# Low parts of the attention's weights: from a subtraction on VectorE to an adding transfer, with a lead of two slots

## The chip, the cores and the metric

The kernel runs on one core of a Trainium2 chip. The metric is the device time of one execution in microseconds; of several executions the median is taken. Each profile is one execution taken by the hardware profiler.

## The reference

Two decoder layers work on one sequence of 512 tokens with 1024 features, all in float32. Each layer has four residual updates in this order; the mixers share one input projection.

```
x = x + 0.5 * swiglu(rms_norm(x, norm_ffn1[l]), ...)
h = rms_norm(x, norm_mix[l])
proj = h @ w_in[l]                      # columns: RWKV-7 | attention | convolution
y_rwkv = rwkv7_mixer(token_shift(proj[..., :1280], shift_mu[l]), ...)
y_attn = attention_mixer(proj[..., 1280:2432], q_norm, k_norm)
y_conv = conv_mixer(proj[..., 2432:], ...)
x = x + concat(y_rwkv, y_attn, y_conv) @ w_out[l]
x = x + 0.5 * swiglu(rms_norm(x, norm_ffn2[l]), ...)
```

The attention has six heads of 64 features and three dilated windows; q and k are normalised per head before the scores. The change concerns the 1152 columns of `w_in` that give the attention's v, k and q.

## The kernel before, in words

**Products in three passes.** The dense products run on TensorE (PE) in float32r. So that little accuracy is lost, each weight tile and each activation is split into a high part, which is the value rounded to float32r, and a low part, which is the value minus its high part. A product is then three matmuls added up in one PSUM bank: high by high, high by low, low by high (`mm3`, lines 124 to 126; for the attention's columns lines 874 to 876, where the low weight stands in line 875 and is the second of the three).

**A slot.** Weights come in slots of up to 128 x 1024 float32, made by `slot` (lines 105 to 119). A slot has three tiles, `raw`, `hi` and `lo`, each out of a ring of three buffers. SyncE (SP) loads `raw` from HBM (L112), ScalarE (ACT) casts it into `hi` (L113). The low part is made in one of two ways. In the plain way VectorE (DVE) subtracts `hi` from `raw` (L118). In the adding way ACT writes the negated high part into `lo` (L115), and a transfer that GpSimd (POOL) issues adds `raw` to it (L116).

```
if add:
    nc.scalar.activation(lo[:, :cols], hi[:, :cols].bitcast(F32), AF.Copy, scale=-1.0)
    nc.gpsimd.dma_start(out=lo[:, :cols], in_=raw[:, :cols], accum_op=ALU.add)
else:
    nc.vector.tensor_tensor(lo[:, :cols], raw[:, :cols], hi[:, :cols].bitcast(F32), op=ALU.subtract)
```

**The feed of the mixer.** The two feed-forward parts of a layer make their slots where they use them, the plain way. The mixer in between takes its slots from the generator `feed`, which knows the whole list in advance: 14 slots of 1024 columns for the RWKV and convolution projections (numbers 0 to 13), 12 slots of 768 columns for the attention (numbers 14 to 25; four each for v, k and q in the order of the list w = 1, 0, 2), and then the slots of the output projection. `WADD` says which numbers are made in the adding way, and up to where the feed stays two slots ahead of the consumer; behind that it stays one ahead:

```
for i, a in enumerate(srcs):
    got.append(self.slot(*a, WADD[0] <= i < WADD[1]))
    if len(got) > (2 if i < WADD[1] else 1):
        yield got.pop(0)
        if len(got) > 1 and i >= WADD[1]:
            yield got.pop(0)
```

**The mixer's order.** Each layer's mixer first runs the columns of slots 0 to 13, and between them the preparation of the RWKV recurrence on DVE, ACT and POOL. Then DVE inverts small triangular blocks in a chain of 60 dependent steps (`inverses`, L585 and L591), ends it with a copy (L594), and SP writes the result to HBM and loads it back rearranged into the tiles `EB` (L564). The recurrence itself goes over eight chunks (`p3`, `p4`, `s1` to `s4`, lines 642 to 706), each a chain of small matmuls with short DVE and ACT steps in between. To keep PE busy between these, dense work is mixed in by `step`: first the attention's columns (`att_cols`), later the attention itself (`att_core`), the convolution's end and the output projection.

`att_cols` goes through three groups of four slots. Each group fills four PSUM banks; for the first two groups ACT then reads each bank twice, a square into one scratch tile (L898) and a scaled copy `nat` (L899), DVE reduces the square (L900, L901), and POOL raises to a power (L902) and multiplies (L904). The next group needs the banks that ACT has read. PE transposes the normalised tiles in `turn` (L854), while the slots after it run. At the lowest priority DVE runs the 30 taps of the convolution (L1008).

**What sets the order.** The program is a list of instructions with priorities in program order; before the run a scheduler orders each engine's queue once, by priority and by when it expects each instruction to be ready. On the chip each queue is worked off in that order.

Of the kernel before, what the change touches and what calls it, by code (L numbers as in the profile page):

```python
# [25 lines left out]
XPAD = 56  # L26
SCRATCH = 2048
CPOS = 4
WADD = (3, 14)
CO = (1, 1)  # L30
TURN = 2
PRE = 8
# [50 lines left out]
class Kern:  # L83
# [202 lines left out]
    def feed(self, srcs):  # L286

        got = []
# [6 lines that stand above are left out]
# [844 lines left out]
```

## Time and profile before

| what | value |
|---|---|
| median of 3 runs | 2071.73 us (2071.52 to 2076.33) |
| the profiled execution | 2076.13 us |
| its span, first to last instruction | 2074.4 us |
| mean granted TensorE clock | 0.989 |
| subtractions on DVE (L118) | 346, 470.6 us |
| negations on ACT (L115) and adding transfers on POOL (L116) | 22 each |

An instruction's time is in us from the start of the span. A line of a timeline has the start, the duration, the engine, the line of the kernel and the tiles written and read; the number in brackets is the idle time of the engine before it and what ended that. PE's matmuls overlap, so their start-to-start distance, not their duration, is what they cost. The first layer's mixer lies at about 340 to 710 us, the second's at about 1370 to 1730.

### The profile page before, as it was taken

How to read it: one execution, taken by the hardware profiler on the slowest of the kernel's cores; microseconds unless marked ns; L12 is line 12 of the kernel's file. 1: busy time of each engine (PE TensorE's matmuls, PEld its weight loads, DVE VectorE, ACT ScalarE, POOL GpSimd, SP SyncE). 2: the span in 40 equal slices, each digit the busy share in tenths (PEclk: the TensorE clock that was granted, in tenths of full speed). 3: DMA queues.
4: the chain of work that ended last, by engine and by line, in shares of the span. 5: the costliest groups of instructions: out<-in, count | busy, mean ns of one | idle time of the engine just before them, and what ended most of it. 6: DMA issues, size and time to landing. Idle time of an engine off the chain costs nothing. (4 is left out here: it accounts for less than half of the span.)

```text
span 2074.4 us, 26095 instructions
## 1 busy us (share of the span) xinstructions
PE 2033.6 (98%) x10406; PEld 1652.5 (80%) x10406; DVE 1095.8 (53%) x1543; ACT 766.4 (37%) x1158; POOL 345.3 (17%) x320
## 2 busy tenths in 40 slices
PE   8999999989999999999999999999999999999999
PEld 6888888767867788888888888887688678888887
DVE  5545433597866545543345454336887664554422
ACT  4323322564365323323233232226634553233221
POOL 3101101232411201110011011002424111110100
PEclk9999999999999999999999999999999899999999
DMA  4232333534312333323323323335333132323332
GB/s 169 92 102 92 97 109 124 131 92 112 85 44 92 103 102 92 100 89 101 97 92 101 102 92 97 112 120 132 95 102 91 34 105 92 100 94 102 99 109 66
DMA packets 85033, 205.34 MB, mean 99 GB/s; under 512 B 26992, under 2 KB 32624, under 8 KB 84912
## 3 DMA queue, kind: packets, MB, share of 16 engines
q1 hardware_dynamic: 81312, 191.79, 29.8%
q0 software_dynamic: 3168, 11.54, 2.8%
q8 instruction: 81, 1.33, 0.3%
q10 hardware_dynamic: 432, 0.36, 0.1%
q14 instruction: 40, 0.33, 0.1%
HBM read 183.47 MB, written 8.65 MB: 93 GB/s over the span
## 5 line engine op out<-in xcount | busy, mean ns | idle before, releaser
L113 ACT CAST hi<-raw 128x1024 fp32r<-128x1024 f32 (+3 forms) x368 | 350.8, 954 | 981.4 <-PE psg L125 854.1
L124 PE MATMUL psg<-xh,hi 128*128 128x512 f32 x1632 | 644.1, 395 | 7.1 <-ACT xh L177 7.1
L125 PE MATMUL psg<-xl,hi 128*128 128x512 f32 x1632 | 643.1, 394 | 5.3 <-DVE xl L178 5.1
L118 DVE TENSOR_TENSOR lo<-raw,hi 128x1024 fp32r<-128x1024 f32 (+4 forms) x346 | 470.6, 1360 | 333.0 <-ACT hi L113 323.6
L126 PE MATMUL psg<-xh,lo 128*128 128x512 f32 x1632 | 640.5, 392 | 0.0
L124 PEld LDWEIGHTS psg<-xh,hi 128*128 128x128 f32 x1632 | 309.2, 189 | 75.1 <-ACT xh L177 7.1
L125 PEld LDWEIGHTS psg<-xl,hi 128*128 128x128 f32 x1632 | 309.5, 190 | 73.3 <-DVE xl L178 8.6
L126 PEld LDWEIGHTS psg<-xh,lo 128*128 128x128 f32 x1632 | 309.1, 189 | 64.8 <-DVE lo L118 0.8
L124 PE MATMUL psg<-ah,hi 128*128 128x512 f32 x704 | 273.9, 389 | 0.0
L125 PE MATMUL psg<-al,hi 128*128 128x512 f32 x704 | 273.9, 389 | 0.0
L126 PE MATMUL psg<-ah,lo 128*128 128x512 f32 x704 | 273.9, 389 | 0.0
L224 POOL TENSOR_TENSOR s<-s,u 128x512 f32<-128x512 f32 x88 | 120.5, 1369 | 800.2 <-ACT hi L113 629.8
L223 DVE TENSOR_TENSOR u<-psg,R 128x512 f32<-128x512 f32 x88 | 60.8, 691 | 265.5 <-PE psg L126 265.2
L124 PEld LDWEIGHTS psg<-ah,hi 128*128 128x128 f32 x704 | 132.2, 188 | 27.5
L126 PEld LDWEIGHTS psg<-ah,lo 128*128 128x128 f32 x704 | 132.2, 188 | 27.5
L125 PEld LDWEIGHTS psg<-al,hi 128*128 128x128 f32 x704 | 132.2, 188 | 27.3
L221 DVE TENSOR_TENSOR g<-psg,R 128x512 f32<-128x512 f32 x88 | 60.8, 690 | 125.5 <-PE psg L126 125.5
L186 POOL TENSOR_TENSOR acc<-acc,sq 128x512 f32<-128x512 f32 x42 | 59.6, 1418 | 381.5 <-ACT sq L185 381.0
L1008 DVE SCALAR_TENSOR_TENSOR cacc<-z,par,cacc 128x482 f32<-128x482 f32 (+14 forms) x120 | 103.8, 865 | 1.5
L129 ACT CAST ah<-s 128x512 fp32r<-128x512 f32 x88 | 54.9, 624 | 121.6 <-POOL s L224 121.6
L130 DVE TENSOR_TENSOR al<-s,ah 128x512 fp32r<-128x512 f32 x88 | 59.8, 679 | 20.9 <-ACT ah L129 20.9
L874 PE MATMUL psg<-hi,xh 128*128 128x384 f32 x192 | 67.4, 353 | 2.3 <-ACT nat L899 2.1
(210 smaller groups left out, 1853.3 us busy)
## 6 DMA issues: line engine op xcount, KB each, us to landing
raw<-in_wgu_dram SPq DMA_DIRECT2D x176, 512.0 KB, 3.5
raw<-in_wd_dram SPq DMA_DIRECT2D x64, 512.0 KB, 3.5
raw<-in_win_dram SPq DMA_DIRECT2D x28, 512.0 KB, 3.5
raw<-in_wd_dram SPq DMA_DIRECT2D x32, 384.0 KB, 3.2
lo<-raw POOLq DMA_DIRECT2D x22, 512.0 KB, 4.4
raw<-in_watt_dram SPq DMA_DIRECT2D x24, 384.0 KB, 3.0
raw<-in_wout_dram SPq DMA_DIRECT2D x28, 192.0 KB, 2.3
xs<-x SPq DMA_DIRECT2D x16, 256.0 KB, 2.0
```

Of the source, the lines that this page charges most:

```text
L113: nc.scalar.copy(hi[:, :cols], raw[:, :cols])
L118: nc.vector.tensor_tensor(lo[:, :cols], raw[:, :cols], hi[:, :cols].bitcast(F32), op=ALU.subtract)
L124: mm(out, lhsT=whi, rhs=xhi, start=first, stop=False)
L125: mm(out, lhsT=whi, rhs=xlo, start=False, stop=False)
L126: mm(out, lhsT=wlo, rhs=xhi, start=False, stop=last)
L130: self.nc.vector.tensor_tensor(lo, src, hi.bitcast(F32), op=ALU.subtract)
L186: nc.gpsimd.tensor_tensor(self.acc, self.acc, sq, op=ALU.add)
L221: nc.vector.tensor_tensor(t[0], p[0], self.R, op=ALU.mult)
L223: nc.vector.tensor_tensor(t[1], p[1], self.R, op=ALU.mult)
L224: nc.gpsimd.tensor_tensor(t[2], t[2], t[1], op=ALU.mult)
L874: mm(o, lhsT=self.xh[kk][:, t], rhs=hi[:, s], start=kk == 0, stop=False)
L1008: nc.vector.scalar_tensor_tensor(a[:, d:], z[:, 0 : T - d], pa("dww", u * CW + j), a[:, d:], op0=ALU.mult, op1=ALU.add)
```

## The change

One constant is changed. Slots 14 to 25, the attention's, are made in the adding way like slots 3 to 13, and the feed keeps its lead of two slots up to number 25 instead of 13. In each of the two layers 12 subtractions of 128 x 768 leave DVE's queue, and 12 negations enter ACT's and 12 adding transfers POOL's. The loads on SP and the matmuls stay the same in number.

```
-WADD = (3, 14)
+WADD = (3, 26)
```

## The prediction

> **What bounds the kernel now.** I read the page first, then the busy time by stretches of the first layer's mixer, then the waits there, and last the timelines of PE, ACT, DVE, POOL and SP through the attention's columns.
>
> ```profile
> span 2074.4 us, 26095 instructions
> ...
> PE 2033.6 (98%) x10406; PEld 1652.5 (80%) x10406; DVE 1095.8 (53%) x1543; ACT 766.4 (37%) x1158; POOL 345.3 (17%) x320
> ...
> DVE  5545433597866545543345454336887664554422
> ```
>
> PE is busy for 98% of the span, so only 2074.4 − 2033.6 = 40.8 us can be won from waits in the whole program. DVE is 53% busy on average, but its row of slices stands at 7 to 9 in the two mixers, where the change acts.
>
> ```profile
> 500.00:510.00 10.00, 10.00 (x59) 10.00 (x58) 9.28 (x23) 1.82 (x3) 0.00 (x0) 1.00 0.29 89
> 510.00:520.00 10.00, 8.72 (x55) 7.69 (x55) 9.76 (x26) 5.63 (x10) 6.65 (x5) 1.00 0.58 167
> ```
>
> ```profile
> PE psg L874 <- ACT nat L899: 1.2, 1, 1.2
> ...
> PE psb L689 <- DVE SVU L681: 0.5, 1, 0.5
> ...
> PE psb L651 <- DVE Z L644: 0.4, 1, 0.4
> ```
>
> The columns are the stretch, the busy time of PE, weight load, DVE, ACT and POOL, the granted clock, and the DMA's share and GB/s. In 500 to 510 us PE runs the first group of attention columns without a gap, DVE is full and ACT and POOL are nearly idle. In 510 to 520 PE loses 1.28 us. The waits (stretch 484 to 560) name nearly all that PE loses there: 1.2 us until ACT has emptied a PSUM bank at the change of groups, and 0.9 us behind DVE in the recurrence. So PE bounds this stage too. The slices show the same hump of DVE twice, so I work the first layer out and double it.
>
> **The change, removed work.** In each layer the twelve attention slots (numbers 14 to 25 of the feed) lose their DVE subtraction and get one more ACT pass and one POOL transfer.
>
> ```profile
> L118 DVE TENSOR_TENSOR lo<-raw,hi 128x1024 fp32r<-128x1024 f32 (+4 forms) x346 | 470.6, 1360 | 333.0 <-ACT hi L113 323.6 <-PE psc L196 9.1
> ...
> L115 ACT ACTIVATE lo<-hi 128x1024 fp32r<-128x1024 f32 x22 | 23.1, 1052 | 0.3
> ...
> L116 POOL DMA_DIRECT2D lo<-raw x22 | 19.4, 882 | 85.9 <-ACT lo L115 81.0 <-PE psb L463 4.4 <-issue 0.4
> ```
>
> ```profile
> 490.69 0.95 DVE L118 TENSOR_TENSOR lo<-raw,hi 128x768 fp32r<-128x768 f32 x1
> ...
> 509.20 0.96 DVE L118 TENSOR_TENSOR lo<-raw,hi 128x768 fp32r<-128x768 f32 x1
> ```
>
> Removed from DVE: 12 × 0.95 = 11.4 us a layer. Five of these subtractions lie between 490.69 and 509.20, in the middle of the inverses' chain; without them the chain ends about 5 × 0.95 = 4.75 us earlier. That matters in one place.
>
> ```profile
> 507.26 0.84 ACT L113 CAST hi<-raw 128x768 fp32r<-128x768 f32 x1 [3.28 <-PE psg L876]
> ...
> 512.32 0.58 ACT L898 ACTIVATE asq<-psg,rnt 128x384 f32<-128x384 f32 x1 [1.40 <-DVE ast L900]
> 512.80 0.57 ACT L899 ACTIVATE nat<-psg,rnt 128x384 f32<-128x384 f32 x1
> 513.26 0.83 ACT L113 CAST hi<-raw 128x768 fp32r<-128x768 f32 x1
> 514.43 0.58 ACT L898 ACTIVATE asq<-psg,rnt 128x384 f32<-128x384 f32 x1 [0.33 <-DVE ast L900]
> ```
>
> ```profile
> 511.22 0.33 PE L874 MATMUL psg<-hi,xh 128*128 128x384 f32 x1
> 511.40 0.33 PE L875 MATMUL psg<-lo,xh 128*128 128x384 f32 x1
> ...
> 513.42 0.45 PE L874 MATMUL psg<-hi,xh 128*128 128x384 f32 x1 [1.17 <-ACT nat L899]
> ```
>
> The second group (slot 18, from 511.22) needs the four banks of the first. ACT's second square waits 1.40 us for DVE's reduction (one scratch tile), DVE is late because it is still in the inverses, and PE waits 1.17 us. With the chain over by about 509 the reduction comes at once: −1.2 us. What is late next is ACT itself, which has two more squares and two more copies to do before PE has its last bank. Of the 0.9 us behind DVE I count half as gone, −0.5: fewer instructions stand ahead of the recurrence's small DVE steps, but the convolution's taps still do.
>
> **Added work.** ACT gets 12 passes that negate the high part. One of 1024 columns takes 1052 ns and the cast of 768 takes 0.84, so I take 0.84 us, 10.1 us a layer, mostly in gaps: ACT is 1.82 us busy of 10 in 500 to 510. At the change of groups it isn't free. The negation of slot 20 goes behind its cast (513.26 + 0.83 = 514.09) and ends at 514.93, so the third square starts then instead of at 514.43: +0.5. Its bounds are 0 and two passes, 1.7.
>
> POOL gets 12 issues of 0.88 us, 10.6 us a layer. Each waits for its negation, and behind it on POOL stand the powers and products that normalise q and k (L902, L904) and the recurrence's products; each such step is up to 0.88 us later. PE reads the first normalised operand only at the transposes (L854, 533.99 below), 9.1 us after the last product has ended at 523.91 + 0.96 = 524.87, so that is 0; without that cover it would cost 0.9 a step.
>
> SP gets nothing new, but its loads wait longer: a raw buffer is now free when the adding transfer has landed, not when a subtraction has read it. Behind SP's load at 516.86 stand the loads for the recurrence, from 517.32.
>
> ```profile
> 516.86 0.35 SPq L112 DMA_DIRECT2D raw<-in_watt_dram  x1
> 517.32 0.37 SPq L564 DMA_DIRECT2D EB<-dE  x1
> ```
>
> If SP keeps that order and slot 20's transfer lands at 519.4 (below), they start 2.6 us late; but the inverses that feed them end 4.75 us earlier, so they can equally go first. I take 0 between −2 and +2.6, since PE has dense columns to run meanwhile.
>
> **Does the low part come in time?** This is the new wait: PE's second matmul of a slot (L875) waits for a transfer.
>
> ```profile
> lo<-raw POOLq DMA_DIRECT2D x22, 512.0 KB, 4.4
> ```
>
> ```profile
> 515.56 2.42 POOL L902 TENSOR_TENSOR ast<-ast,mh 128x6 f32<-128x6 f32 x1 [0.67 <-DVE ast L901]
> 518.06 1.35 POOL L904 TENSOR_TENSOR nat<-nat,ast 128x384 f32<-128x384 f32 x1
> 519.37 1.74 POOL L902 TENSOR_TENSOR ast<-ast,mh 128x6 f32<-128x6 f32 x1
> 521.19 0.94 POOL L904 TENSOR_TENSOR nat<-nat,ast 128x384 f32<-128x384 f32 x1
> ...
> 523.91 0.96 POOL L904 TENSOR_TENSOR nat<-nat,ast 128x384 f32<-128x384 f32 x1
> ...
> 553.77 0.83 POOL L904 TENSOR_TENSOR nat<-nat,ast 128x384 f32<-128x384 f32 x1
> ```
>
> ```profile
> 522.99 0.34 PE L875 MATMUL psg<-lo,xh 128*128 128x384 f32 x1
> ...
> 533.99 0.66 PE L854 MATMUL psc<-tab,nat 128*128 128x128 f32 x4
> ...
> 556.31 0.33 PE L875 MATMUL psg<-lo,xh 128*128 128x384 f32 x1
> ```
>
> Where ACT and POOL are free, take slot 19, whose cast starts at 507.26 as soon as PE releases the buffer (so the lead in the feed moves nothing here: the ring of three buffers already sets the cast). Cast and negation end at 508.94, POOL issues, and 4.4 us later, 513.3, the low part is there. A slot is 24 matmuls, started 0.175 us apart (511.22 and 511.40 above), 4.2 us of PE, so slot 19 can't start before 511.40 + 4.2 = 515.6: 2.3 us to spare. I use the 4.4 of 512 KB as the upper end for these 384 KB. [...]
>
> Slot 20 is the tight one. Its negation ends at 514.93 and PE wants it at 522.99 (slot 20's second matmul). Issued before POOL's power at 515.56 it lands at 519.4, in time. Issued after the product at 518.06 (ends 519.41) it lands at 523.8, 0.8 late; after that at 521.19 (ends 522.13) at 526.5, 3.5 late; after the last (ends 524.87) at 529.3, 6.3 late. Which place the scheduler gives it, no trace shows. On ACT the cast of that slot, which comes later in the program, was put into the first gap between two squares, and the gap on POOL at 514.9 to 515.6 is like it. I take the middle of the first two, +0.4. Slot 24 has the same neighbours at the second change of groups, where POOL's last product ends at 554.60: issued behind it, it lands at 559.0, 2.7 after PE wants it (556.31); issued one pair of steps earlier it is in time, which I take, 0.
>
> **Sum.** A layer: −1.2 − 0.5 + 0.5 + 0.4 = −0.8 us; both −1.6. The profiled execution took 2076.13 us (span 2074.4 and 1.7 around it), so 2074.5 by that one; it is itself 4.4 above the median of 2071.73, from which I get 2070.1. With all gains and no cost (−2.1 a layer) 2067.5; with none and slot 20 at 0.8, ACT's 1.7 (+2.5 a layer) 2076.7. About 0.3%, 6.2 us, is what a measurement of this kernel can tell from no change; all of that is inside.
>
> **Rivals.** *Slot 20 behind POOL's queue (slower).* If the issue stands behind three or four powers and products, PE stalls for 3.5 or 6.3 us. And a stall near 3 us has a price after it:
>
> ```profile
> 450.00:460.00 10.00, 7.05 (x50) 5.52 (x49) 8.65 (x8) 3.99 (x7) 6.88 (x5) 0.99 0.32 79
> 460.00:470.00 10.00, 9.48 (x46) 7.03 (x44) 9.80 (x14) 6.34 (x9) 4.01 (x4) 0.84 0.30 60
> ```
>
> PE idles 2.95 us and in the next ten the granted clock is 0.84, so another 1.6 us are lost. [...] So a layer is 3.5 + 1.6 − 1.2 = +3.9 or 6.3 + 1.6 − 1.2 = +6.7, in all +7.8 or +13.4: 2079.5 or 2085.1. With slot 24 behind its queue as well, 2.7 a layer come on top. It decides once the issue comes after about 521 us. For it: the powers are earlier in the program, and POOL is backlogged from 515.56 on. Against: the gap before that, and that the squares come earlier once the inverses do. Chance 0.14.
>
> *The half-clock stretches go (faster).* Later in each mixer PE has poorly filled stretches:
>
> ```profile
> 590.00:595.00 5.00, 5.00 (x17) 3.36 (x18) 2.09 (x6) 0.81 (x2) 1.52 (x2) 0.50 0.17 36
> ```
>
> ```profile
> 1600.00:1610.00 10.00, 10.00 (x108) 6.49 (x109) 6.66 (x28) 5.97 (x22) 1.97 (x4) 0.83 0.13 42
> 1610.00:1620.00 10.00, 10.00 (x95) 6.68 (x96) 5.25 (x15) 4.16 (x12) 1.17 (x2) 0.83 0.01 2
> ```
>
> They lose 2.5 and 2 × 1.7 us, 5.9 in all. If the recurrence starts up to 4 us earlier and mixes with more dense columns, these could vanish: −1.6 − 5.9 = −7.5, 2064.2. For it: the load that starts it waits for the inverses. Against: the matmuls and their order in the program stay. Chance 0.18.
>
> *Nothing moves.* DVE's time wasn't what PE waited for, the reduction stays where it was, the transfers are hidden: 0, 2071.7. Chance 0.20.
>
> **How the numbers follow.** The forecast has 0.48. With the third rival 0.68 lies within 0.3%; 0.18 is faster and 0.14 slower. The likeliest time is 2070.1. The range takes in the faster rival's middle and the first of the slower one's two prices: 2063 to 2080.
>
> **What would show it.** L118 down by 24, L115 and L116 up by 24 each; PE's wait on nat gone or under 0.5; no wait of L875 on the transfer in slots 14 to 19. I am wrong on slot 20 if the wait for a low part (L116) is seen on PE by more than 1 us, and wrong on the cause if the inverses end earlier and PE still waits on nat for over a microsecond.

## The result, and the profile after

| | before | after |
|---|---|---|
| median of 4 runs each, same chip | 2071.62 us (2070.81 to 2076.33) | 2086.22 us (2085.88 to 2086.71) |
| the profiled execution | 2076.13 us | 2085.88 us |
| PE idle in its span (span minus PE's busy time) | 40.8 us | 48.2 us |

The kernel became slower by 14.6 us: ratio 1.0062, 95% interval 1.005 to 1.0074. The prediction, 2070.1 us with a range of 2063 to 2080, was wrong.

From the page of after: the span, the busy times, the line of the subtractions, and the DMA issues of the adding transfers (count, KB each, median us from issue to landing).

```profile
span 2084.1 us, 26155 instructions
...
PE 2035.9 (98%) x10406; PEld 1655.3 (79%) x10406; DVE 1073.5 (52%) x1519; ACT 784.9 (38%) x1182; POOL 359.7 (17%) x344
...
L118 DVE TENSOR_TENSOR lo<-raw,hi 128x1024 fp32r<-128x1024 f32 (+4 forms) x322 | 445.5, 1384 | 340.9 <-ACT hi L113 331.7
...
lo<-raw POOLq DMA_DIRECT2D x24, 384.0 KB, 4.4
```

The edit did what it says: 24 subtractions fewer, DVE 22.3 us less busy, 24 transfers more. PE, the engine that bounds the kernel, idles 7.4 us more, and its own busy time rises by 2.3 us with the same 10406 matmuls; the run's mean granted clock is 0.987 instead of 0.989. The two make the 9.7 us between the two spans; before's profiled run was itself 4.5 us above the median of 2071.62. Over all runs, a run's span times its mean granted clock (an estimate of what it would take at full clock) rose from 2052.7 us on average (the 23 runs of before beside the first four experiments) to 2059.4 (4 runs), and the rest, lost to the clock, from 18.7 to 25.0. So about half of the loss is waiting and half is clock; a wait at half clock counts half to each in this sum, and the clock is recorded to three digits, which leaves about 1 us of a run either way open.

After by stretches: the two stretches that the prediction quoted, and three in the last group of columns. Columns: PE, weight load, DVE, ACT, POOL, granted clock, DMA share, GB/s.

```profile
500.00:510.00 10.00, 10.00 (x60) 10.00 (x59) 9.14 (x29) 4.17 (x6) 2.46 (x3) 1.00 0.68 154
510.00:520.00 10.00, 7.73 (x47) 6.13 (x45) 9.89 (x20) 5.25 (x10) 6.56 (x7) 1.00 0.74 176
550.00:555.00 5.00, 2.87 (x30) 2.48 (x26) 0.00 (x0) 1.74 (x3) 4.92 (x5) 1.00 0.55 98
555.00:560.00 5.00, 3.79 (x40) 3.44 (x41) 2.34 (x6) 0.63 (x2) 2.06 (x4) 0.53 0.77 163
560.00:565.00 5.00, 5.00 (x25) 4.77 (x23) 0.43 (x1) 0.41 (x1) 0.00 (x0) 0.79 0.43 115
```

The same place in before:

```profile
550.00:555.00 5.00, 4.47 (x54) 3.95 (x53) 4.91 (x8) 0.68 (x3) 4.44 (x4) 1.00 0.15 25
555.00:560.00 5.00, 5.00 (x29) 4.28 (x27) 4.85 (x10) 0.53 (x2) 1.34 (x2) 1.00 0.38 98
```

In 550 to 555 DVE, which was full before, does nothing at all, POOL is full, and PE runs dry. Behind that the granted clock is 0.53 and 0.79 for ten microseconds. By finer stretches it stands at 0.50 from 555.29 to 562.12; dense products start 0.32 us apart there (559.52 to 561.76) and 0.17 before (550.79 to 552.53). PE works for 5.91 us of the stretch, so by the granted clock about 3.0 us more are lost, an estimate. The waits of after in 484 to 600 us say on whom:

```profile
DVE yb L821 <- POOL gst L191: 7.5, 2, 6.0
...
PE psb L651 <- DVE Z L644: 3.3, 1, 3.3
...
PE psb L642 <- DMA EB<-dD: 1.8, 2, 1.2
...
PE psg L874 <- ACT nat L899: 0.8, 1, 0.8
...
PE psg L875 <- DMA lo<-raw: 0.5, 1, 0.5
```

Before had 0.4 in the second line, 1.2 in the fourth, and the third and fifth not at all. The first line had been there as well:

```profile
DVE yb L821 <- POOL gst L191: 4.4, 2, 2.9
```

That line is the one that I had passed over. `gst` is the statistic of the group norm on the recurrence's output (`gn`, called by the mixer between the chunks): DVE reduces it, ACT squares (L818), POOL raises it to the power (L191, in the helper `rsqrt`), and DVE multiplies (L821). The chain, from the timelines of POOL, DVE and PE of after:

```profile
548.53 1.32 POOL L902 TENSOR_TENSOR ast<-ast,mh 128x6 f32<-128x6 f32 x1
549.93 0.83 POOL L904 TENSOR_TENSOR nat<-nat,ast 128x384 f32<-128x384 f32 x1
550.70 0.91 POOL L116 DMA_DIRECT2D lo<-raw  x1
551.36 1.64 POOL L902 TENSOR_TENSOR ast<-ast,mh 128x6 f32<-128x6 f32 x1
553.07 0.83 POOL L904 TENSOR_TENSOR nat<-nat,ast 128x384 f32<-128x384 f32 x1
553.87 1.31 POOL L191 TENSOR_TENSOR gst<-gst,mh 128x6 f32<-128x6 f32 x1
...
549.09 0.17 DVE L190 TENSOR_SCALAR gst<-gst 128x6 f32<-128x6 f32 x1
555.21 0.56 DVE L821 TENSOR_TENSOR yb<-yc,gst 128x384 f32<-128x384 f32 x1 [5.95 <-POOL gst L191]
555.80 0.36 DVE L644 TENSOR_TENSOR Z<-psb,tab 128x192 f32<-128x192 f32 x1
...
556.21 0.90 PE L651 MATMUL psb<-EB,Z 64*64 64x64 f32 x12 [3.34 <-DVE Z L644]
```

The same chain in before, on POOL and DVE:

```profile
547.66 0.83 POOL L904 TENSOR_TENSOR nat<-nat,ast 128x384 f32<-128x384 f32 x1
548.45 1.32 POOL L191 TENSOR_TENSOR gst<-gst,mh 128x6 f32<-128x6 f32 x1
549.74 1.32 POOL L902 TENSOR_TENSOR ast<-ast,mh 128x6 f32<-128x6 f32 x1
...
545.23 0.32 DVE L190 TENSOR_SCALAR gst<-gst 128x6 f32<-128x6 f32 x1
...
549.80 0.56 DVE L821 TENSOR_TENSOR yb<-yc,gst 128x384 f32<-128x384 f32 x1 [2.86 <-POOL gst L191]
...
551.12 0.36 DVE L644 TENSOR_TENSOR Z<-psb,tab 128x192 f32<-128x192 f32 x1
```

In before the power stands behind the second of POOL's four pairs of power and product (L902, L904; the groups come in the order k, q, v, so these pairs are q's, of slots 18 to 21). DVE waits 2.86 us for it, which PE covers with dense columns. In after it stands behind the fourth pair and one adding transfer. Its operand is there at 549.26, POOL starts it at 553.87. DVE takes its queue in order: PE's last product for the recurrence's `Z` (L644), which has nothing to do with the group norm, ends at 550.24, and `Z` starts at 555.80, behind L821 (555.21). PE's queue has its order too: the dense columns ahead of L651 end 3.34 us before `Z` lets L651 start, and the next ones stand behind it (558.72). Both layers show the same (6.7 us on L651 in the whole program, 1.0 in before). In the first layer the columns of the last group, from their first matmul to their last, take 34.6 us and not 29.5, the second group takes 1.3 longer, and the whole mixer from the first attention matmul to the next norm 208.2 and not 200.3.

### The profile page after: what moved, and what is told of

Same layout as the page of the kernel before. It is cut to its first block, busy times and chain, and to the rows that moved or that the text cites. A ratio compares the mean times of both kernels' runs of the same rounds, so it can differ in the third digit from the quotient of the medians.

```text
span 2084.1 us, 26155 instructions
## 1 busy us (share of the span) xinstructions
PE 2035.9 (98%) x10406; PEld 1655.3 (79%) x10406; DVE 1073.5 (52%) x1519; ACT 784.9 (38%) x1182; POOL 359.7 (17%) x344
## 5 line engine op out<-in xcount | busy, mean ns | idle before, releaser
L118 DVE TENSOR_TENSOR lo<-raw,hi 128x1024 fp32r<-128x1024 f32 (+4 forms) x322 | 445.5, 1384 | 340.9 <-ACT hi L113 331.7
L1008 DVE SCALAR_TENSOR_TENSOR cacc<-z,par,cacc 128x482 f32<-128x482 f32 (+14 forms) x120 | 99.3, 828 | 1.9
```

Of the source, the lines that this page charges most:

```text
L1008: nc.vector.scalar_tensor_tensor(a[:, d:], z[:, 0 : T - d], pa("dww", u * CW + j), a[:, d:], op0=ALU.mult, op1=ALU.add)
```

## The experiments

**Theory Q**: what costs is the place of the group norm's power in POOL's queue (and of its square in ACT's); DVE's queue waits behind it, PE waits for `Z`, and half-clock follows. **Theory T**: the adding transfers cost by themselves, as traffic and as late low parts. In all kernels below `WADD` is a list of slot numbers that are made in the adding way, and `LEAD` the number up to which the feed stays two slots ahead. "Group norm first" or "late" moves the priority of the one call of `gn`, and so the place that the scheduler gives all its instructions. Differences are medians against the kernel before on the same chip, which ran 23 times beside lead_only, neg_dve, add_only and gn_first, 35 beside the next four, 23 beside the next three, 13 beside all_two and 23 beside the last three. The ratio and its interval come from all runs and are not the quotient of the two medians, so the two columns can differ by a microsecond or two; an interval reaches 2 to 3 us either way.

| run | us over before | ratio, 95% interval |
|---|---|---|
| lead_only | +9.7 | 1.0044 [1.0028, 1.0060] |
| neg_dve | +9.6 | 1.0037 [1.0024, 1.0050] |
| add_only | +6.1 | 1.0034 [1.0018, 1.0050] |
| gn_first | +4.2 | 1.0023 [1.0009, 1.0037] |
| lead_gn_first | +1.2 | 1.0008 [0.9998, 1.0018] |
| before_gn_first | −0.1 | 1.0004 [0.9993, 1.0015] |
| gn_first_skip | +1.5 | 1.0010 [1.0000, 1.0020] |
| gn_first_six | +1.0 | 1.0002 [0.9992, 1.0013] |
| gst_late | +11.9 | 1.0057 [1.0044, 1.0071] |
| six_two | −5.2 | 0.9971 [0.9959, 0.9983] |
| two_gn | −3.0 | 0.9985 [0.9975, 0.9996] |
| all_two | +9.9 | 1.0041 [1.0024, 1.0057] |
| two_1819 | +5.6 | 1.0026 [1.0014, 1.0037] |
| two_2024 | +21.5 | 1.0105 [1.0089, 1.0121] |
| two_late | −5.0 | 0.9979 [0.9968, 0.9990] |

**lead_only**: the lead without the transfers.

```
WADD = 3..13;  LEAD = 26        # before: 3..13 and 14; the change: 3..25 and 26
```

> Only the lead of two slots up to slot 25; the attention's low parts stay subtractions. Theory Q (the group norm's power, L191, now stands in POOL's queue behind all four powers and products of q; DVE waits for it, and PE for DVE): in this kernel's POOL order it stands behind all four pairs too, so it loses most of what the change lost: 5 to 11 us over the 2071.6 of before, DVE's wait yb on gst 4 to 6 us in the first layer, PE's wait on Z 2 us or more. Theory T (the adding transfers themselves: DMA traffic beside the loads of the inverses, and low parts that come late): there are none in the attention here, so 0 us, 2070 to 2073.

It lost 9.7 us with not one adding transfer for the attention in it. Its timelines of POOL, DVE and PE:

```profile
552.78 1.32 POOL L191 TENSOR_TENSOR gst<-gst,mh 128x6 f32<-128x6 f32 x1
...
554.13 0.56 DVE L821 TENSOR_TENSOR yb<-yc,gst 128x384 f32<-128x384 f32 x1 [4.98 <-POOL gst L191]
...
555.13 0.58 PE L651 MATMUL psb<-EB,Z 64*64 64x64 f32 x12 [4.02 <-DVE Z L644]
```

It is the same picture as after. ACT's timeline shows where it begins, first in before, then in lead_only:

```profile
543.00 0.52 ACT L818 ACTIVATE yb<-yc 128x384 f32<-128x384 f32 x1
543.42 0.83 ACT L113 CAST hi<-raw 128x768 fp32r<-128x768 f32 x1
```

```profile
542.98 0.83 ACT L113 CAST hi<-raw 128x768 fp32r<-128x768 f32 x1
...
544.64 0.54 ACT L818 ACTIVATE yb<-yc 128x384 f32<-128x384 f32 x1
```

With the longer lead the cast of a slot to come is taken ahead of the group norm's square, one pair of the attention's goes ahead as well, and on POOL the power falls behind all four pairs. T expected no loss here, so it can't be the whole cause.

**neg_dve**: the change with its lead and negations, but DVE adds instead of a transfer.

```
-nc.gpsimd.dma_start(out=lo, in_=raw, accum_op=ALU.add)      # slots of 768 columns
+nc.vector.tensor_tensor(lo, raw, lo, op=ALU.add)
```

> As the change, but slots 14 to 25 get raw added to the negated high part by a DVE addition instead of a transfer: ACT's extra passes and the lead stay, POOL's issues and the transfers are gone. Theory Q: the group norm's power stands behind three of the four pairs in POOL's queue, one less than in the change, so 2 to 7 us over before. Theory T: 0 us, 2070 to 2073. If ACT's passes at the two changes of groups are the cost: 2 to 4 us over before, with PE's wait on nat longer than the 1.2 us of before.

The power stands behind three pairs (550.62), DVE waits 3.5 us, and PE 2.9 us on another step of DVE's (SVU, L689). It lost 9.6 us, more than the 2 to 7 that Q had expected, and PE's wait on `nat` is 0.7 us, so ACT's passes at the changes of groups aren't what costs; by span times clock, on average over its runs, 2.3 us are waits and 9.0 went to the clock. Why this run lost so much clock stays open.

**add_only**: the transfers without the lead.

```
WADD = 3..25;  LEAD = 14
```

> Adding transfers for slots 3 to 25, with the lead as before (two up to slot 13, then one). Theory Q: the group norm's power stands behind three pairs and no issue stands between, so the wait of DVE is about 3 us shorter than in the change: 4 to 9 us over before. Theory T: the transfers are all there, so as the change, 2085 to 2088.

It lost 6.1 us, in Q's range and not in T's, but the waits don't bear Q out alone. The power is behind three pairs again (DVE's wait 4.4), yet PE waits only 0.7 us for `Z`; the transfers show more, in the first layer 1.7 us for low parts and 1.9 for the loaded `EB`.

**gn_first**: the whole change, group norm first.

```
-gn = self.gn(l, c - 1, B["Y"], ...)
+tc.cur_priority -= 3000; gn = self.gn(l, c - 1, B["Y"], ...); tc.cur_priority += 3000
```

> The change with the group norm's instructions at a higher priority, so that its power stands behind the first of the four pairs in POOL's queue. Theory Q: PE's wait on Z of 3.3 us and the half clock behind it go, in both layers; what is left is the wait on the loads of the inverses (1.8) and on slot 20 (0.5): 2 to 5 us over before, 2074 to 2077. Theory T: nothing changes, 2084 to 2088.

Of the 14.6 us, 4.2 are left, as Q expected. DVE's longest wait on the power is 1.5 us, PE's on `Z` 1.2.

**lead_gn_first** and **before_gn_first**: the same edit on lead_only and on the kernel before.

> The lead of two alone, with the group norm's instructions at a higher priority: its power then stands behind the first of q's four pairs in POOL's queue. Theory Q (the place of that power is all that the lead costs): the 10 us of the lead alone go, within 2 us of before; PE's wait on Z falls from 4.0 us to under 1. A rival, that the lead costs by moving other things too (casts earlier on ACT, PSUM banks): 5 us or more over before stay.

> The kernel before with nothing but the group norm at a higher priority. Theory Q: DVE's wait for the power (2.9 us) shrinks to under 1.5, but PE hardly waited for it, so 0 to 1.5 us faster. If the place of the power decides the granted clock too, up to 4 us faster.

The lead's 9.7 us shrink to 1.2, whose interval includes no change, and the edit by itself brings nothing to the kernel before (−0.1). So it is a repair and no separate gain, and the group norm's place is worth 9.7 − 1.2 = 8.5 us beside the lead and 14.6 − 4.2 = 10.4 in the change, each a difference of two figures with intervals of 2 to 3 us either way. The edit moves the whole call of `gn`: that it is the power among its steps is read from the traces (DVE's longest wait on it is 6.0 us in after and 1.5 in gn_first).

**gn_first_skip** and **gn_first_six**: gn_first with slots 18 and 19 subtracted again, and with all from 18 on subtracted.

```
WADD = 3..17, 20..25            # gn_first_skip
WADD = 3..17                    # gn_first_six
```

> As the change with the group norm first, but slots 18 and 19, whose transfers run beside the store and load of the inverses, are subtracted. Theory T (their traffic delays those loads): PE's wait on the loads of EB, 1.9 us a layer, falls under 0.5, and the time is 2 to 4 us below that of the group norm first alone. If the traffic isn't the cause, no difference.

> Of the attention's slots only 14 to 17 get adding transfers; lead two throughout, group norm first. DVE is freed while it inverts, no transfer of the attention runs beside the loads of the inverses, and none stands among POOL's powers. Theory Q with T: no cost is left and the inverses end some 3 us earlier, so 0 to 3 us faster than before, 2070 to 2073. If ACT's negations or the lead cost by themselves: 3 us or more over before.

PE's wait for `EB` is gone in both and the loss falls from 4.2 to 1.5 and 1.0. That is no clear step, since the intervals overlap, and gn_first_six isn't the 0 to 3 us faster that was expected; PE's wait on `nat` is 2.9 to 3.0 us in the first layer and now the largest.

**gst_late**: the kernel before, with the group norm's call later by 300 steps of priority. It was to give Q's dose by itself.

> The kernel before, with the group norm's instructions at a lower priority, so that its power stands behind all four of q's pairs in POOL's queue, as in the change and in the lead alone; no transfer, no lead. Theory Q: DVE waits 4 to 6 us for the power instead of 2.9, PE 2.5 us or more for Z in each layer, and the time is 5 to 11 us over before. A rival, that the lead or the transfers are needed for the loss: within 2 us of before.

The size was a little over Q's 5 to 11 us (+11.9), the way was not Q's. The power stands behind all four pairs (551.45), but the rest of the group norm moved as well, so that DVE's queue waits only 2.8 us. The loss lies later, in these waits of 600 to 660 us:

```profile
PE psb L833 <- DVE yb L821: 3.6, 1, 3.6
PE psg L124 <- ACT mix L129: 1.8, 1, 1.8
```

Before has 0.5 and 0.3 there. A late group norm is dear in two ways, then, by DVE's queue or by its own readers. As a proof of the first way this run missed.

**six_two** and **two_gn**: the squares (L898) get a second scratch tile in turn, so that ACT's next square needn't wait for DVE's reduction; six_two on gn_first_six, two_gn on before with the group norm first.

```
-sq = self.nrm.tile([P, W], F32, tag="R", ...)
+sq = self.nrm.tile([P, W], F32, tag=("R", "sq")[i % 2], ...)
```

> The version with slots 14 to 17 only and the group norm first, with two scratch tiles for the squares of k and q instead of one, so that ACT's next square needn't wait for DVE's reduction. If that wait is what PE loses at the changes of groups (2.9 us a layer there), PE's wait on nat falls under 1.5 and the time is 2 to 5 us below before; if ACT's own four squares and copies are the limit, within 1 us of the version with one tile.

> The kernel before with two scratch tiles and the group norm first; no lead, no transfer for the attention. If the scratch tile is what PE waits for: 1 to 3 us below before. If ACT is the limit: within 1 us of it.

Both beat the kernel before, by 5.2 and 3.0 us. PE's wait on `nat` in the first layer is 1.2 us in six_two (2.9 without the second tile) and 0.2 in two_gn. Since two_gn has no adding transfer for the attention, 3.0 of the 5.2 us don't come from them. The other 2.2 aren't clear of the noise (the intervals overlap), and in span times clock the two agree, 2050.6 and 2050.7.

**all_two**: six_two with all twelve slots added, which is the change with both repairs.

> The change whole (adds in slots 3 to 25, lead of two slots), with the group norm put ahead of the pairs and two scratch tiles for the squares, so that it differs from six_two only in slots 18 to 25, which are made by adding transfers and not by subtractions. Theory Q (the change loses only through the place of the group norm's power in POOL's queue) expects six_two's time within 2 us, that is 4 to 7 us under the kernel before, because nothing else of the change costs anything. Theory T (the transfers beside the inverses' store and load cost as well) expects PE to wait again for the loaded EB by about 1.9 us a layer, as in the gn_first run, and so a time 3 to 5 us above six_two: within 2.5 us of the kernel before.

This was the surprise: 9.9 us slower than before, against both expectations. Q is no full account of these transfers. The kernel differs from gn_first (+4.2) only in the second scratch tile, which had gained 6.2 us between gn_first_six and six_two. The scheduler has now put the issues of slots 20 and 24 behind all four pairs of the group before theirs (POOL 526.30 and 556.78). In the first layer PE waits 2.2 us for the low part of slot 24 (560.65; slot 20's is covered by steps of the recurrence), 1.9 for `EB`, and already in the preparation ahead of the attention 2.1 us (L492 behind the step GG on DVE) instead of before's 0.5. So the transfers were taken apart, always on six_two. **Theory C**: what costs is the transfers of slots 18 and 19 beside the store and load of the inverses. **Theory P**: the place of slots 20 and 24 in POOL's queue, behind the pairs of the group before (slot 20 is the third of its group and slot 24 of the next; where the expectation below calls them the first of a group, that is a slip).

**two_1819**, **two_2024** and **two_late**:

```
WADD = 3..17, 18, 19
WADD = 3..17, 20, 24
WADD = 3..17, 21, 22, 23, 25
```

> As six_two (adds in slots 3 to 17, group norm first, two scratch tiles, lead of two slots to number 25), and slots 18 and 19 added as well: their transfers run while the inverses are stored and loaded. Theory C (the transfers' own cost is that collision) expects PE to wait for the loaded EB by 1 to 2 us a layer and a time 3 to 5 us above six_two, so 0 to 2 us under the kernel before. Theory P (the own cost is the place of slots 20 and 24 behind POOL's powers and products) expects no wait for EB over 0.5 us and six_two's time, 4 to 6 us under before.

> As six_two, and slots 20 and 24, the first of the second and third group, added as well: their issue stands among POOL's powers and products. Theory P expects PE to wait for a low part by about 2 us a layer, as in all_two, with half-clock behind it, and a time 5 to 10 us above six_two: 0 to 5 us over the kernel before. Theory C expects six_two's time within 2 us, 4 to 6 us under before.

> As six_two, and slots 21, 22, 23 and 25 added as well, that is all of all_two but 18, 19, 20 and 24. Theories C and P both expect six_two's time within 2 us, 4 to 6 us under the kernel before. If the transfers cost as such, wherever they stand, this has half of all_two's eight more and half of its 14 us above six_two: about 2 us over before.

Four transfers a layer in two_late cost nothing that these runs can tell: −5.0 against six_two's −5.2. So at these places in the queues the transfers as such, their negations on ACT and their issues on POOL show no cost. Slots 20 and 24 cost 21.5 + 5.2 = 26.7 us (each run against before on its own chip), where P had expected 5 to 10. POOL and PE in two_2024:

```profile
525.02 0.96 POOL L904 TENSOR_TENSOR nat<-nat,ast 128x384 f32<-128x384 f32 x1
525.93 0.92 POOL L116 DMA_DIRECT2D lo<-raw  x1
...
529.85 0.69 PE L875 MATMUL psg<-lo,xh 128*128 128x384 f32 x1 [6.02 <-DMA lo<-raw]
```

Slot 20's issue stands behind the last product and PE waits 6.0 us for it. Behind it comes half-clock (two_2024 by stretches):

```profile
525.00:530.00 5.00, 0.15 (x1) 0.15 (x1) 1.80 (x3) 0.00 (x0) 1.83 (x2) 0.54 0.62 150
530.00:535.00 5.00, 5.00 (x38) 3.89 (x40) 1.00 (x2) 0.32 (x1) 0.00 (x0) 0.50 0.24 79
```

In the whole program these waits for a low part are 16.9 us in four places, against 4.6 in all_two. Slots 18 and 19 cost 5.6 + 5.2 = 10.8 us. PE waits 3.7 us for `EB` in two places, as C says, but the time is twice what C had given it at most (3 to 5 us); 1.5 us more than in six_two are lost in the preparation (L492 behind the step GG), and by span times clock, on average over the runs, 2.6 are waits and 7.2 clock. So C has its place shown and only part of its price. Why a transfer after 500 us changes PE's waits at 465, and when a wait is followed by more half-clock, stays open; the scheduler places all of the mixer's instructions at once, and no run here separates that. Nor do the prices add up: 10.8 + 26.7 + 0.2 is 37.7 us, and all_two, which has all eight slots, is 9.9 + 5.2 = 15.1 us above six_two. A price here belongs to a whole queue as the scheduler dealt it, not to a slot.

## Why the prediction was wrong, step by step

**The step that failed** is the one on POOL's queue: "each such step is up to 0.88 us later. PE reads the first normalised operand only at the transposes [...] so that is 0; without that cover it would cost 0.9 a step." I listed who reads the normalised tiles and found them covered, which holds (L854 shows no wait). I didn't list what else is in that queue. The group norm's power stands there too, and its reader is DVE, whose queue holds the recurrence's steps. And I counted a delay of one issue per step, while the scheduler dealt the queue out anew: the power went from behind the second pair to behind the fourth and a transfer. The step put the cost at nothing; with the group norm first 10.4 of the 14.6 us go (8.5 of 9.7 in lead_only).

**The lead.** "So the lead in the feed moves nothing here: the ring of three buffers already sets the cast" was the second failure. It moves the cast's place in ACT's queue ahead of the group norm's square, and lead_only shows 9.7 us.

**The removed subtractions, −1.2 on `nat`.** The chain of inverses did end earlier (first layer, 508.92 against 512.86, 3.9 of the expected 4.75 us; DVE's row of slices stands at 7 to 9 in only three slices of each mixer, not throughout as the prediction has it), but the reduction didn't come at once. DVE in after:

```profile
508.92 1.12 DVE L594 COPY Et<-Ei 96x1024 f32<-96x1024 f32 x1
509.96 2.22 DVE L1008 SCALAR_TENSOR_TENSOR cacc<-z,par,cacc 128x482 f32<-128x482 f32 x3
512.09 0.54 DVE L900 TENSOR_REDUCE ast<-asq 128x6 f32<-128x384 f32 x1
```

Three taps of the convolution were put in front of it, so it came at 512.09 (before 511.68), and PE still waited 0.85 us in the first layer (before 1.17) and 1.7 in the second (before 0.9): 2.5 against 2.1 in all. The sign that the prediction named for a wrong cause, over a microsecond although the inverses end earlier, is there in the second layer and just missed in the first. A second scratch tile removes what the reduction blocks (two_gn: 0.2). The other two terms of this sum came out otherwise as well. The −0.5 for the waits behind DVE became a loss, since L651's wait went from 0.4 to 3.3 us. The +0.5 for ACT's negation of slot 20 was 0: it stands behind the third square and copy (515.34), and the third square starts at 514.40.

**EB: 0, between −2 and +2.6.** The copy of the inverses starts 3.9 us earlier and PE nevertheless waited 1.8 us, inside the bounds (which the prediction's best and worst sums had left out). Most of what was won was lost in the transfers: the store (`dD`) is issued at 510.06 instead of 513.96, but it took 6.8 us instead of 3.8, so it landed only 0.9 us earlier, and the recurrence's first product (L642) starts at 520.29 instead of 522.45. DMA issues of after in 504 to 522 us, then of before in 508 to 524 (count, KB, median us to landing):

```profile
lo<-raw POOLq DMA_DIRECT2D x3, 384.0 KB, 6.9
...
dD<-Et SPq DMA_DIRECT2D x1, 384.0 KB, 6.8
```

```profile
dD<-Et SPq DMA_DIRECT2D x1, 384.0 KB, 3.8
```

**Slots 14 to 19 in time, 2.3 us to spare**: not so for slot 18, the one ahead of the slot that I had worked out. Its issue starts at 505.11, the first matmul that needs it at 512.02 after a wait of 0.53: 6.9 us and not 4.4, with the loads and the store beside it. In the second layer PE doesn't wait for it.

**Slot 20, +0.4**: it was issued behind the second pair (519.00), the second of the prediction's four places, which was to make it 0.8 us late. It landed after 4.2 us, and no wait of PE's is seen on it. **Slot 24, 0**: no wait is seen on it either. **The slower rival** ("slot 20 behind POOL's queue") had the time nearly right (2085.1 for 2086.2) and the mechanism wrong for this kernel, so that nearness is luck. The price of its stall is borne out in another kernel, two_2024: 6.3 us predicted for an issue behind the last product, 6.0 measured. Its term for the clock, 1.6 us a stall, is right for the stall in after's second layer (1.7) and too small for the first (3.0).

**The faster rival** didn't come; on average the clock lost 6.3 us more than before. **The chances** gave slower 0.14. All my rivals looked for what the new instructions do; none asked what the scheduler would do to the old ones.

## What to carry to other kernels

Where a scheduler orders in-order queues, the cost of an instruction in a queue with time to spare is who stands behind it (here 10.4 of the 14.6 us), and a wait that is harmless now (DVE on POOL, 2.9 us) is the first place to look, since it tells how little has to slip. Changes of this kind can be tried piece by piece: of twelve slots, eight (14 to 17, 21 to 23 and 25) showed no cost where the group norm goes first and the squares get a second tile (−5.0 us in all, of which the tile and the place of the group norm alone give 3.0). Two collide with a store and two are issued behind a full queue. But every edit lets the scheduler deal the queues anew, so the pieces don't add up, and the whole has to be measured as well.

## What the runs showed of the hardware

In after an adding transfer's time differs more with what runs beside it than with its size. One of 384 KB takes 4.4 us in the median, about as one of 512 KB does (4.5 there, 4.4 in before). Those of slots 16 and 17 take 3.8 and 4.3 us, those of slots 18 and 19, with the loads and the store of the inverses beside them, 6.9 and 7.9.

Each stall of PE below came with a stretch at a granted clock of 0.50, but its length alone doesn't set the price. What the clock took while PE was at work is an estimate, half of PE's busy time in the stretch; measured, dense products start 0.32 us apart in after's first stretch and 0.17 ahead of it, a little under twice. The bounds of two_2024's stretch are worked out from slices of 5 us (0.54, 0.50 and 0.94 from 525 to 540).

| run, end of the stall | stall, us | stretch at 0.50 | its length, us | lost at work, us |
|---|---|---|---|---|
| before, 459.03 | 2.95 | 459.75 to 463.17 | 3.4 | 1.7 |
| after, 556.21 | 3.34 | 555.29 to 562.12 | 6.8 | 3.0 |
| after, 1592.17 | 3.35 | 1592.94 to 1596.36 | 3.4 | 1.7 |
| two_2024, 529.85 | 6.02 | 525.4 to 535.6 | 10.2 | 2.9 |

Two stalls of the same length in after cost 3.0 us in one layer and 1.7 in the other, and in two_2024 the clock is at half 1.6 us after PE's last matmul has ended (523.83). In lead_only, behind the stall of 4.02 us that ends at 555.13, dense products start 0.32 us apart from 557.80 to 558.76 and 0.17 from 559.04 on. What sets how long such a stretch lasts, no run here tests.

Over all runs of a kernel the loss to the clock lies between 16.7 us (six_two) and 31.0 us (two_2024) on average, and it follows the waits only loosely: gst_late and neg_dve lose 27.8 and 27.7 with fewer waits than the change, which loses 25.0.
